# Attention scores from split fp32r operands, and output weight blocks split earlier

## The chip, the cores and the metric

One core of one Trainium2 chip runs one program. The metric is the device time of one execution in microseconds (us); lower is better. TensorE is called PE here, its weight load PEld, VectorE DVE, ScalarE ACT, GpSimd POOL and SyncE SP. In the profile's notation `128x512` is partitions by elements, `128*128` the rows and columns of the PE array that a matmul uses, and L496 is line 496 of the kernel before.

## The reference

A trunk of two layers over 512 tokens of width 1024. Each layer normalises, projects with one combined matrix, runs three mixers side by side (differential attention, a short convolution, gated linear attention), projects their concatenation with `w_out`, and adds a mixture of 16384 single-neuron experts. The change touches the differential attention and the loading of `w_out`:

```python
q, k = rope(da_q), rope(da_k)                    # (B, S, 4 heads, 2 maps, 64)
s = einsum('bqhmd,bkhmd->bhmqk', q, k) / 8       # causal
p = softmax(s)
a = p[:, :, 0] - lam * p[:, :, 1]
o = einsum('bhqk,bkhe->bqhe', a, v)              # then RMSNorm per head
...
x = x + concat([o_da, o_sc, o_g]) @ w_out        # (512, 1024) @ (1024, 1024)
x = x + peer(rmsnorm(x), ...)
```

## The kernel before

**Number formats.** Most large products are made in a split form: a float32 operand is rounded to fp32r (`hi`, a copy on ACT) and the remainder is stored in fp32r too (`lo = src - hi`, a subtraction on DVE). `split` (L88) does both. `mm3` (L82) then issues three matmuls, hi·hi, hi·lo and lo·hi. The attention scores are the exception: they are plain float32 matmuls, which the trace shows as two matmul records for each product.

**The mixer of a layer** (`mixer`, L230) streams `w_in` in slabs of 256 columns. `slab` loads four raw pieces with SP and splits each; `across` multiplies the slab with the normalised activations (48 matmuls of 512 columns) and yields two results. The last three slabs, at columns 2048, 1792 and 1536, belong to the short convolution, and the attention is written between them:

1. After gated linear attention has ended and its pool is closed, the pool `attn` opens on the right side of the memory. It holds two query tiles `qz0`, `qz1` (zeroed by POOL, L378), the exponentials `e`, their transposes `aT` and the head outputs `ho`.
2. `attend(0)`, slab 2048, `attend(1)`, slab 1792, and within slab 1536 the queries of block 2 and the first two heads of its scores.
3. The pool `wout` opens where the slabs lay. Eight blocks of 128 rows of `w_out` are loaded and split in the order 6, 7, 4, 5, 0, 1, 2, 3; `attend(2)` and `attend(3)` follow, then `out_proj` for four token blocks, each with the norm of the next stage behind it.

**Scores.** A query block `tb` of 128 tokens sees `nk = (tb+1)*128` keys. `turned_queries` (L483) copies the 64 rows of map m into `qz[r, :, m]`; the other 64 rows stay zero, so a product over all 128 rows gives the scores of one map alone. `head_weights` (L489) makes, for each of 4 heads and 2 maps, the product `qz[:, h, m]` by `kT[:, h, 0:nk]` (L496), adds the causal mask by a bfloat16 matmul over the last 128 columns (L497), takes the row maximum on DVE (L498), and exponentiates on ACT (L503). `diff_attention` (L511) transposes the difference of the maps on PE (L524), copies it out (L526) and multiplies it with the values (L528). There are 32 score products in a layer, 8 of each width 128, 256, 384 and 512.

**Order.** The program is traced in the order above and a scheduler then writes a fixed list for each engine from its own estimates of durations. Each engine works through its list in order; a matmul that waits holds up those behind it. PE interleaves slab matmuls with the attention in that list. DMAs are issued by SP (weights), by ACT, and by POOL (the rotary pieces, L469 to L481).

## Time and profile before

| | us |
|---|---|
| median of 3 runs | 2874.95 |
| lowest, highest | 2874.74, 2875.98 |
| profiled execution, whole time | 2872.9 |
| profiled execution, span of its instructions | 2871.1 |
| PE busy in it | 2844.5 |
| DVE busy in it | 2454.2 |

The profile is one execution. Its granted TensorE clock is 0.999. The attention lies at about 145 to 266 us of the span in the first layer and at about 1570 to 1691 us in the second; everything else is the slabs before it and, for the greater part of the span, the experts. A timeline row gives the start, the time from the first to the last end of a run of like instructions, the engine, the line, the operation, and how often. Because matmuls overlap, the time that one takes of PE is read from the distance of two starts.

### The profile page before, as it was taken

To read this page: it belongs to the slowest core of one execution; us is meant where nothing else is said; L and a number is where in the kernel's file an instruction comes from. 1 tells how busy PE (TensorE), PEld (TensorE's weight loads), DVE (VectorE), ACT (ScalarE), POOL (GpSimd) and SP (SyncE) were. 2 spreads that over 40 slices of the span, in tenths; PEclk is the share of its full clock that TensorE was granted. 3 is DMA by queue.
4 is the path that set the end of the run, shared out by engine and by line. 5 is a ranking of instruction groups with operands and counts; after the bars stand their busy time and mean duration, and the time that the engine had idled before them with its cause. 6 is when DMAs were issued, how large, how long until landed. Compare 5 with 4: busy or idle time off the path is not lost.

```text
span 2871.1 us, 44951 instructions
## 1 busy us (share of the span) xinstructions
PE 2844.5 (99%) x16328; PEld 2529.5 (88%) x16328; DVE 2454.2 (85%) x4874; ACT 1274.1 (44%) x1922; POOL 844.8 (29%) x715
## 2 busy tenths in 40 slices
PE   8999999999999999999999999999999999999998
PEld 7878899999998998888888788999999999988887
DVE  6675989997998899888966769999979888998888
ACT  6253346675333333333453533556743333333333
POOL 1200002211665665222112000121126665552221
PEclk9999999999999999999999999999999999999999
DMA  4322259998999999999733122699989999999995
GB/s 133 95 64 99 89 167 324 324 311 304 377 383 374 388 372 365 367 360 362 269 99 92 63 92 90 209 313 326 316 302 384 384 382 386 375 363 368 360 361 223
DMA packets 346048, 790.50 MB, mean 275 GB/s; under 512 B 32384, under 2 KB 193056, under 8 KB 341728
## 3 DMA queue, kind: packets, MB, share of 16 engines
q1 hardware_dynamic: 159472, 424.18, 40.9%
q0 software_dynamic: 87136, 312.85, 29.6%
q10 hardware_dynamic: 99216, 50.60, 5.9%
q8 instruction: 128, 2.10, 0.3%
q14 instruction: 96, 0.79, 0.1%
HBM read 705.39 MB, written 78.91 MB: 273 GB/s over the span
## 4 chain that ended last, share of the span: by engine, by line
PE 70%; DVE 4%; ACT 1%; issue 1%; DMA 0%; DVEq 0%; ACTq 0%
PE pv L85 12%; PE pv L86 12%; PE pv L84 12%; PE psh L84 8%; PE psh L85 8%; PE psh L86 8%; PE psg L1318 1%; PE psp L85 1%; PE psp L86 1%; PE psp L84 1%; PE psq L84 1%; PE psq L85 1%; PE psq L86 1%; PE pss L790 1%; PE pso L85 0%
## 5 line engine op out<-in xcount | busy, mean ns | idle before, releaser
L86 PE MATMUL pv<-vh,wl 128*128 128x512 f32 x1500 | 584.7, 390 | 0.0
L85 PE MATMUL pv<-vl,wh 128*128 128x512 f32 x1500 | 584.6, 390 | 0.0
L84 PE MATMUL pv<-vh,wh 128*128 128x512 f32 x1500 | 583.6, 389 | 0.0
L854 POOL DMA_INDIRECT row<-in_u_rows,idx x256 | 361.7, 1413 | 341.9 <-DVE row L860 224.3
L854 POOL DMA_INDIRECT row<-in_v_rows,idx x256 | 316.9, 1238 | 485.8 <-DVE yacc L867 449.7
L1020 DVE TENSOR_TENSOR vl<-vraw,vh 128x1024 fp32r<-128x1024 f32 x250 | 305.9, 1223 | 91.6 <-issue 79.1
L860 DVE SCALAR_TENSOR_TENSOR row<-row,xg 128x1024 f32<-128x1024 f32 x320 | 382.5, 1219 | 0.3 <-DMA row<-in_u_rows,idx 0.2
L1024 ACT CAST vh<-vraw 128x1024 fp32r<-128x1024 f32 x250 | 263.1, 1052 | 193.8 <-PE pv L86 184.8
L1032 ACT CAST wh<-g 128x384 fp32r<-128x384 f32 x250 | 128.3, 513 | 471.5 <-DVE g L1188 458.4
L84 PE MATMUL psh<-ahi,uwb 128*128 128x352 f32 x1024 | 334.0, 326 | 0.0
L84 PE MATMUL psh<-ahi,uwa 128*128 128x352 f32 x1024 | 333.5, 326 | 0.0
L86 PEld LDWEIGHTS pv<-vh,wl 128*128 128x128 f32 x1500 | 281.6, 188 | 58.6
L85 PEld LDWEIGHTS pv<-vl,wh 128*128 128x128 f32 x1500 | 281.6, 188 | 57.4
L84 PEld LDWEIGHTS pv<-vh,wh 128*128 128x128 f32 x1500 | 281.6, 188 | 57.3
L85 PE MATMUL psh<-alo,uwa 128*128 128x352 f32 x1024 | 330.8, 323 | 0.0
L85 PE MATMUL psh<-alo,uwb 128*128 128x352 f32 x1024 | 330.6, 323 | 0.0
L86 PE MATMUL psh<-ahi,uwa 128*128 128x352 f32 x1024 | 327.2, 320 | 0.0
L86 PE MATMUL psh<-ahi,uwb 128*128 128x352 f32 x1024 | 326.9, 319 | 0.0
L867 DVE SCALAR_TENSOR_TENSOR yacc<-row,wk,yacc 128x1024 f32<-128x1024 f32 x254 | 325.2, 1280 | 2.0
L771 ACT ACTIVATE ht<-psh 128x352 f32<-128x352 f32 x256 | 119.1, 465 | 456.6 <-PE psh L86 435.1
L756 DVE TENSOR_TENSOR uwa<-uraw,uwa 128x1024 fp32r<-128x1024 f32 x144 | 175.7, 1222 | 67.1 <-ACT uwa L755 61.2
L756 DVE TENSOR_TENSOR uwb<-uraw,uwb 128x1024 fp32r<-128x1024 f32 x144 | 175.9, 1222 | 63.0 <-ACT uwb L755 54.3
(384 smaller groups left out, 5783.0 us busy)
## 6 DMA issues: line engine op xcount, KB each, us to landing
uraw<-in_peer_u SPq DMA_DIRECT2D x256, 512.0 KB
vraw<-in_v_rows SPq DMA_DIRECT2D x252, 512.0 KB
G<-stg ACTq DMA_DIRECT2D x48, 1024.0 KB
g<-G SPq DMA_DIRECT2D x30, 1536.0 KB
H<-ht SPq DMA_DIRECT2D x144, 176.0 KB
ht<-H SPq DMA_DIRECT2D x144, 176.0 KB
wraw<-in_w_in SPq DMA_DIRECT2D x84, 256.0 KB
uraw<-in_peer_w_q SPq DMA_DIRECT2D x32, 512.0 KB
```

The source lines that it names most:

```text
L84: mm(ps, ah, bh, start=first, stop=False)
L85: mm(ps, ah, bl, start=False, stop=False)
L86: return mm(ps, al, bh, start=False, stop=last)
L756: self.before, self.last = self.last, pin(nc.vector.tensor_tensor(lo, src, hi.bitcast(F32), op=OP.subtract))
L771: pin(nc.scalar.activation(hs[c][:, 0:TD], ps, AF.Gelu))
L790: nc.tensor.matmul(pss[:, tb], qt[:, tb * P:tb * P + P], keys[:, w], start=True, stop=True)
L854: nc.gpsimd.indirect_dma_start(out=r, out_offset=None, in_=ins[name], in_offset=bass.IndirectOffsetOnAxis(ap=at, axis=0))
L860: nc.vector.scalar_tensor_tensor(r, r, 1.0, xg, op0=OP.mult, op1=OP.mult, accum_out=out)
L867: nc.vector.scalar_tensor_tensor(acc, r, w, acc, op0=OP.mult, op1=OP.add)
L1020: return pin(nc.vector.tensor_tensor(like(lo, src), src, like(hi.bitcast(F32), src), op=OP.subtract))
L1024: pin(nc.scalar.copy(vh[c], vs[c]))
L1032: pin(nc.scalar.copy(like(wh[c], ws[c]), ws[c]))
```

## The change

The scores no longer use float32 matmuls. The keys are split into `kh` (rounded, a copy on ACT) and `kl` (the remainder, on DVE). DMAs issued by POOL then stack them: after them the upper 64 rows of `kh` hold the low part of map 0's keys, and a new tile `kr` holds the rounded keys of map 1 in its upper rows and their low part in its lower rows. `turn_q` rounds the queries of a block into both halves of `qz` (copy on ACT, then a DMA into the other 64 rows) and keeps the remainder in `ql` (DVE). A score is then two fp32r matmuls and the mask: `qz[:, h, m]` (128 rows) by the stacked keys, which gives the rounded queries times rounded and low keys together, and `ql[r, h]` (64 rows) by the 64 rows of rounded keys. The zeroing of `qz` goes. Blocks 0 and 1 are turned before `attend(0)`, blocks 2 and 3 after `attend(1)`.

The key tiles and three buffers for output weight blocks lie in a new pool, `early`, with a filler tile `line` that sets where `kh` begins. The first of the three buffers serves as `kl` first. Blocks 6, 7 and 4 of `w_out` are loaded through a tile in the place of `qT` and split there, behind slab 1536 in program order; the other five go to the pool `wout`. The norm's scratch tiles take places of `attn` instead of a pool of their own.

```diff
+                kl = new_w(kp, 3).rearrange("p a (b t) -> p (a b) t", t=T)
+                kp.tile([P, 40], F32, name="line")
+                kh = kp.tile([P, 4, T], F32R, name="kh")
+                for i in range(0, 4, 2):
+                    h = slice(i, i + 2)
+                    nc.scalar.copy(kh[:, h], kT[:, h])
+                    nc.vector.tensor_tensor(kl[:, h], kT[:, h], kh[:, h].bitcast(F32), op=OP.subtract)
+                kr = mp.tile([P, 4, T], F32R, tag="kT", name="kr")
+                for i in range(0, 4, 2):
+                    h = slice(i, i + 2)
+                    nc.gpsimd.dma_start(kr[64:128, h], kh[64:128, h])
+                    nc.gpsimd.dma_start(kr[0:64, h], kl[64:128, h])
+                    nc.gpsimd.dma_start(kh[64:128, h], kl[0:64, h])
+                keys = (kh, kr)
...
+                turn_q(0)
+                turn_q(1)
                 attend(0)
...
                 attend(1)
+                turn_q(2)
+                turn_q(3)
...
+                korder = (6, 7, 4, 5, 0, 1, 2, 3)
+                wr = mp.tile([P, 2, D], F32, tag="qT", name="woraw")
+
+                def load_w(k, pool, bufs):
+                    raw = wr[:, len(wo) % 2]
+                    wo[k] = new_w(pool, bufs)
+                    nc.sync.dma_start(raw, ins["w_out"][L, k * P:(k + 1) * P, :])
+                    self.split(wo[k][:, 0], wo[k][:, 1], raw)
+
+                for k in korder[:3]:
+                    load_w(k, kp, 3)
+
             with tc.tile_pool(name="wout", bufs=1, reuse_waits="tile") as op_:
...
-                for k in korder:
-                    raw = wr.pop(0) if wr else op_.tile([P, D], F32, tag="woraw", name="woraw", bufs=2)
-                    nc.sync.dma_start(raw, ins["w_out"][L, k * P:(k + 1) * P, :])
-                    self.split(wh[:, k], wl[:, k], raw)
+                for k in korder[3:]:
+                    load_w(k, op_, 5)
...
-    def turned_queries(self, tb, qT, qz):
+    def turned_queries(self, tb, qT, qz, ql):
         s = slice(tb * P, tb * P + P)
-        for m in range(2):
-            r = slice(64 * m, 64 * m + 64)
+        rows = [slice(64 * m, 64 * m + 64) for m in range(2)]
+        for m, r in enumerate(rows):
             self.nc.scalar.copy(qz[r, :, m], qT[r, :, s])
+            self.nc.gpsimd.dma_start(qz[rows[1 - m], :, m], qz[r, :, m])
+            self.nc.vector.tensor_tensor(ql[r], qT[r, :, s], qz[r, :, m].bitcast(F32), op=OP.subtract)
...
-            nc.tensor.matmul(ps[:, 0:nk], qz[:, h, m], kT[:, h, 0:nk], start=True, stop=False)
+            r = slice(64 * m, 64 * m + 64)
+            nc.tensor.matmul(ps[:, 0:nk], qz[:, h, m], keys[m][:, h, 0:nk], start=True, stop=False)
+            nc.tensor.matmul(ps[:, 0:nk], ql[r, h], keys[m][r, h, 0:nk], start=False, stop=False)
             nc.tensor.matmul(ps[:, tb * P:nk], self.identb, self.causal, start=False, stop=True)
```

## The prediction

> **What bounds the kernel now.** I read the page first, then the busy time by stretches of the attention, then PE's timeline inside it.

> ```profile
> span 2871.1 us, 44951 instructions
> PE 2844.5 (99%) x16328; PEld 2529.5 (88%) x16328; DVE 2454.2 (85%) x4874; ACT 1274.1 (44%) x1922; POOL 844.8 (29%) x715
> ...
> 185.40:199.10 13.70, 13.08 (x61) 8.74 (x59) 9.86 (x23) 5.30 (x14) 0.00 (x0) 1.00 0.00 0
> 199.10:233.70 34.60, 34.38 (x179) 25.21 (x180) 27.13 (x67) 22.49 (x56) 0.00 (x0) 1.00 0.33 108
> ...
> sum 120.80, PE 119.91 PEld 91.31 DVE 81.44 ACT 60.38 POOL 0.51; mean PE 23.98 PEld 18.26 DVE 16.29 ACT 12.08 POOL 0.10
> ...
> sum 120.80, PE 119.76 PEld 91.01 DVE 81.35 ACT 60.16 POOL 0.51; mean PE 23.95 PEld 18.20 DVE 16.27 ACT 12.03 POOL 0.10
> ```

> The columns after the stretch are its length and the busy time of PE, PEld, DVE, ACT and POOL. The two sums are the same five stretches in the first and the second layer, from the end of gated linear attention to the first expert query. PE is busy 119.9 of 120.8 us: PE is the bound, and the stage's time is what PE's list costs. Waits can be gained only where PE is idle, 0.9 and 1.0 us a layer. So the question is what a score costs on PE before and after. Each score ends in its mask (L497), so the distance of two mask matmuls is the period of one score:

> ```profile
> 149.70 0.22 PE L497 MATMUL pss<-causal,identb 128*128 128x128 bf16 x1
> 149.76 0.44 PE L496 MATMUL pss<-kT,qz 128*128 128x128 f32 x2
> 150.03 0.22 PE L497 MATMUL pss<-causal,identb 128*128 128x128 bf16 x1
> ...
> 161.57 0.22 PE L497 MATMUL pss<-causal,identb 128*128 128x128 bf16 x1
> 161.63 0.65 PE L496 MATMUL pss<-kT,qz 128*128 128x256 f32 x2
> 162.11 0.22 PE L497 MATMUL pss<-causal,identb 128*128 128x128 bf16 x1
> ...
> 186.06 0.22 PE L497 MATMUL pss<-causal,identb 128*128 128x128 bf16 x1
> ...
> 186.81 0.22 PE L497 MATMUL pss<-causal,identb 128*128 128x128 bf16 x1
> ...
> 204.88 0.22 PE L497 MATMUL pss<-causal,identb 128*128 128x128 bf16 x1
> 204.94 1.08 PE L496 MATMUL pss<-kT,qz 128*128 128x512 f32 x2
> 205.85 0.22 PE L497 MATMUL pss<-causal,identb 128*128 128x128 bf16 x1
> ```

> The periods are 0.33, 0.54, 0.75 and 0.97 us for 1 to 4 blocks of 128 keys: 0.12 fixed (mask, and the weight load behind it that the short mask does not hide) and 0.213 per block.

> **The change part by part: a score on PE.** An fp32r matmul of known cost is that of the slabs:

> ```profile
> 135.07 0.28 PE L86 MATMUL psp<-wh,alo 128*128 128x256 f32 x1
> 135.18 0.28 PE L84 MATMUL psp<-wh,ahi 128*128 128x256 f32 x1
> ...
> 159.76 0.39 PE L84 MATMUL psp<-ahi,wh 128*128 128x512 f32 x1
> 159.99 0.39 PE L85 MATMUL psp<-alo,wh 128*128 128x512 f32 x1
> ```

> It takes 0.11 us at 256 and 0.23 at 512 columns, a quarter of float32's 0.43 and 0.85. Two passes instead of the float32 product would cost 0.107 per block of keys instead of 0.213 (at one block a weight load of about 0.11 is not covered, so nothing is gained). That alone gives periods of 0.33, 0.33, 0.44 and 0.55, a gain of 0, 0.21, 0.31 and 0.42, times 8 each 7.5 us a layer and 15.0 in all.

> But the second pass uses 64 rows of the array, the first and the mask 128. The kernel before has such neighbours in gated linear attention (psu has 64 rows, pst 128):

> ```profile
> 1508.81 1.13 PE L627 MATMUL pst<-qs,ks 128*128 128x256 f32 x4
> 1509.87 0.70 PE L665 MATMUL psu<-gv,kdT 64*128 64x256 f32 x2
> 1510.49 1.99 PE L627 MATMUL pst<-qs,ks 128*128 128x256 f32 x8
> 1512.42 0.70 PE L665 MATMUL psu<-gv,kdT 64*128 64x256 f32 x2
> 1513.04 1.13 PE L627 MATMUL pst<-qs,ks 128*128 128x256 f32 x4
> ...
> 1510.49 1.59 PEld L627 LDWEIGHTS pst<-qs,ks 128*128 128x128 f32 x8 [0.33 <-issue]
> 1512.41 0.29 PEld L665 LDWEIGHTS psu<-gv,kdT 64*128 64x128 f32 x2 [0.33 <-DVE at L629]
> ```

> Two pst products (x4 records) hold PE for 1.06 us, four (x8) for 1.93: 0.435 each and 0.19 left over for every stay in one row mode. One psu product of the same width holds it 0.62, again 0.435 and 0.19. PEld shows why: the first load after a change of mode starts only with the slot itself, while inside a mode loads run ahead. So a change of mode costs about 0.195 us, part drain, part a load that nothing covers. A new score has two, into the 64-row pass and back to the mask.

> [...]

> The mask's weights are shorter to load:

> ```profile
> L496 PEld LDWEIGHTS pss<-kT,qz 128*128 128x128 f32 x128 | 20.3, 190 | 8.2 <-issue 2.9 <-ACT e L503 2.2 <-ACT mh L553 0.5
> L497 PEld LDWEIGHTS <-identb 128*128 128x128 bf16 x64 | 6.3, 99 | 4.4 <-issue 1.9
> ```

> 99 against 190 ns, so I take 0.105 for the way back (0.195 is its upper end) and 0.30 for both. The periods become 0.53, 0.63, 0.74 and 0.85; against before +0.20, +0.09, -0.01 and -0.12, times 8 a loss of 1.3 us a layer, **+2.6** in all. With 0.195 on the way back it is 32 × 0.09 = 2.9 a layer more, +8.4; without the two changes of mode it is -15.0.

> One width has no row: no fp32r matmul here has under 256 columns. Proportional cost (nearest rows, which I take) is in the sum. The other end is the float32 cost per pass, 0.213 instead of 0.053: 2 × 0.16 × 8 = 2.6 a layer, +5.1.

> **What stands ahead of the first score.** Before, the scores began at 148.91:

> ```profile
> 144.37 1.03 PE L718 MATMUL htr<-ident,o 128*128 128x128 f32 x8
> 145.16 0.48 PE L84 MATMUL psp<-ahi,wh 128*128 128x512 f32 x1
> ...
> 148.91 0.38 PE L496 MATMUL pss<-kT,qz 128*128 128x128 f32 x2
> ...
> L89 ACT CAST woh<-woraw 128x1024 fp32r<-128x1024 f32 x16 | 16.9, 1055 | 7.3 <-DMA woraw<-in_w_out 7.2
> L90 DVE TENSOR_TENSOR wol<-woraw,woh 128x1024 fp32r<-128x1024 f32 x16 | 19.6, 1222 | 2.8 <-ACT woh L89 2.6
> L487 ACT COPY qz<-qT 64x512 f32<-64x512 f32 x16 | 9.9, 619 | 1.5 <-PE pss L496 1.2
> ...
> 100.44 2.13 POOL L481 DMA_DIRECT2D qT<-rot  x4 [12.29 <-issue]
> ...
> 106.58 1.07 POOL L469 DMA_DIRECT2D rot<-kT  x2 [2.98 <-DMA qT<-rot]
> ```

> The key tiles lie where gated linear attention lay, whose last transposes end at 145.4. Then come two copies (ACT, 1.06 each) and two subtractions (DVE, 1.22 each), of the size of L89 and L90, and six POOL DMAs of about 0.53 each to issue. The third of each three overwrites what the first reads, so it waits for that to land; POOL's queue is in order, and behind it stand the other half's three, then four for the queries of blocks 0 and 1. From the rotary rows a landing takes some 4 us (the last of four was issued near 102.0, and the next writer of the same tile started at 106.58). So the first scores come at 145.4 + 1.1 + 1.2 + 0.5 + 4 + 0.5 + 4, about 157, those of heads 2 and 3 near 161: 8 to 12 us late. PE's cover is slab 2048, 48 matmuls of 0.23 from 145.16 to 156.2, then slab 1792, 11 us more. It holds if PE's list puts slab matmuls ahead of the scores; where the scheduler thought the DMAs quicker, PE stands still for the difference, 0 to 5 us a layer. I take 1 a layer, **+2.0**.

> [...]

> **The rest, under cover.** DVE gets 8 remainders of queries (half the width of the L90 row, so about 0.61 each) and the keys' 2.4, some 7 us a layer, and ACT gets 2.1. By the sums of the stretches DVE is idle for 39 of 120.8 us and ACT for 60, so both have the room. The 3 earlier blocks move 3.7 us of DVE and 3.2 of ACT out of 199 to 234, where DVE is busy 27.1 of 34.6. What can that free? Only PE's idle time there, 0.6 us ahead of 199.1 and 0.2 after it:

> ```profile
> 199.09 0.94 PE L528 MATMUL po<-va,aT 128*128 128x128 f32 x6 [0.62 <-ACT aT L526]
> ```

> It waits for a transpose's copy, not for a block, so I take 0 and keep -0.8 a layer as the end. Three SP loads of `w_out` move ahead, waiting for the last reader of `qT`; nothing stands behind them on SP but the other blocks. Two POOL clearings go, from a queue that delays nobody. The norm's scratch in places of `attn` waits for the last exponentials, which end before the norm starts. The head outputs' tiles move down into the place of a raw block, so the second block of query weights may be split only when `out_proj` ends, one split (1.06 and 1.22 us) ahead of its use; the first block's query matmuls, 24 of 0.11 us, lie between, so I count 0. The alignment filler costs nothing by itself.

> **Sum.** +2.6 + 2.0 = +4.6 us. The sum is made against the profiled execution, 2872.9 us with 1.8 around its span; the median of the runs shown, 2874.95, lies 2.05 above it, so the forecast is 2874.95 + 4.6 = **2879.5**.

> **The rivals.** *No drain for these matmuls* (faster): in the slab stream loads run ahead of matmuls and nothing is lost, so if fp32r passes of 64 and 128 rows follow each other like that, 15.0 us go and 2.0 come: 2862. Against it: every psu slot in both layers shows the 0.19. *The narrow fp32r pass runs at float32 speed* (slower): +5.1 on the forecast, 2884.6; it decides as soon as a 128-column pass takes over 0.09 us, since 0.04 × 32 makes the 1.2 us that are missing to the bound of slower. For it: no row; against it: 0.11 at 256 columns. *PE stands at the first scores* (slower): 5 us a layer instead of 1, +8: 2887.5; it decides from 1.6 a layer. For it: the landing of 4 us; against it: 11 us of slab 1792 that could go first.

> **How the numbers follow.** About 0.2% (5.7 us) is what a measurement of this kernel can tell from no change. Forecast 0.38, its own range 2876 to 2884 (the way back at its upper end, or the idle time gained); no drain 0.30; narrow pass 0.18; stand at the first scores 0.14. Faster is the no-drain case: 0.30. Same is 0.29 of the forecast's 0.38 and 0.03 of the others. Slower is the rest, 0.38. The range goes from 2860 (no-drain without the waits) to 2888.

> **What would show it.** Right: rows of `pss` with 64*128, an idle PEld ahead of each, mask-to-mask periods near 0.63 and 0.85 at two and four blocks. Wrong: periods near 0.33 and 0.55 (no drain); fp32r pss records of one block with starts 0.2 apart (narrow pass); a PE row with several us of idle released by a DMA into `qz` or `kh` after 150 (stand). A changed pv or psh mean would show the addresses, which I price at nothing, at work.

## The result: 2895.2 us, slower, and more than the range allowed

| | before | changed |
|---|---|---|
| median, us | 2874.84 (6 runs, 2874.07 to 2875.98) | 2895.16 (6 runs, 2888.29 to 2900.25) |
| ratio, 95% interval | | 1.0069, 1.0054 to 1.0084 |
| profiled execution, whole time | 2872.9 | 2888.29 |
| mean granted clock over all its runs | 0.999 (profiled) | 0.991 to 0.996 |

The change costs 20.3 us where 4.6 were forecast; the time lies above the range's end of 2888. It also spreads over 12 us where the kernel before spreads over 2, and its three longest executions (2896.9 to 2900.3) have the lowest clocks (0.991 and 0.992). The profile of the changed kernel is its fastest execution, 15.4 us over the profiled one of before. The head of its page, and the two stretches by busy time, from the end of gated linear attention to the first expert query:

```profile
span 2886.5 us, 45042 instructions
PE 2854.1 (99%) x16328; PEld 2535.5 (88%) x16328; DVE 2460.7 (85%) x4894; ACT 1278.3 (44%) x1926; POOL 854.0 (30%) x739
```

```profile
146.11:273.20 127.09, 123.79 (x596) 93.52 (x595) 84.31 (x226) 61.90 (x162) 8.53 (x15) 0.97 0.35 91
1576.70:1705.90 129.20, 124.90 (x595) 94.47 (x594) 84.23 (x226) 61.75 (x162) 8.53 (x15) 0.96 0.34 89
```

Each stretch took 120.80 before. So 6.3 and 8.4 us of the 15.4 are in the attention, the rest in a slightly later start. PE is idle 3.3 and 4.3 us there (0.9 and 1.0 before), and the seventh column behind the stretch is new: the granted clock is 0.97 and 0.96, not 1.00. PE's timeline of the scores, layer one:

```profile
161.98 0.30 PE L528 MATMUL pss<-kh,qz 128*128 128x128 f32 x1 [0.74 <-DMA kh<-wk]
162.21 0.32 PE L529 MATMUL pss<-kh,ql 64*128 64x128 f32 x1
162.47 0.23 PE L530 MATMUL pss<-causal,identb 128*128 128x128 bf16 x1
...
163.00 0.23 PE L530 MATMUL pss<-causal,identb 128*128 128x128 bf16 x1
...
165.11 0.39 PE L84 MATMUL psp<-ahi,wh 128*128 128x512 f32 x1
167.01 0.33 PE L528 MATMUL pss<-kh,qz 128*128 128x128 f32 x1 [1.51 <-ACT e L536]
...
168.29 0.30 PE L556 MATMUL atr<-ident,e 128*128 128x128 f32 x1 [0.70 <-DVE st L538]
...
203.92 0.23 PE L530 MATMUL pss<-causal,identb 128*128 128x128 bf16 x1
...
204.68 0.23 PE L530 MATMUL pss<-causal,identb 128*128 128x128 bf16 x1
...
215.02 0.23 PE L530 MATMUL pss<-causal,identb 128*128 128x128 bf16 x1
...
215.90 0.23 PE L530 MATMUL pss<-causal,identb 128*128 128x128 bf16 x1
```

The periods, mask to mask, are 0.53, 0.76 and 0.88 for one, three and four blocks, as forecast (0.53, 0.74, 0.85). What was not forecast stands in the brackets. The first score waited for a DMA into `kh` for only 0.74; the longer waits are 1.51 for an exponential and 0.70 behind it (2.71 and 0.70 in the second layer). Why the exponential was late is in the rows of the other engines, and in the tables of DMA issues (KB each, median us to landing), of 145 to 172 us and then of two short windows, 148 to 149.5 and 155.6 to 157:

```profile
148.70 2.01 ACT L383 CAST kh<-kT 128x1024 fp32r<-128x1024 f32 x2
...
151.79 1.26 POOL L516 DMA_DIRECT2D qz<-qz  x2 [18.03 <-ACT qz L515]
153.03 0.56 POOL L388 DMA_DIRECT2D kr<-kh  x1
...
157.12 0.51 POOL L390 DMA_DIRECT2D kh<-wk  x1 [2.50 <-DMA kr<-kh]
...
164.39 0.62 ACT L89 CAST wh<-wraw 128x512 fp32r<-128x512 f32 x1 [2.84 <-DMA wraw<-in_w_in]
165.04 0.69 DVE L90 TENSOR_TENSOR wl<-wraw,wh 128x512 fp32r<-128x512 f32 x1 [2.77 <-ACT wh L89]
165.65 0.68 DVE L531 TENSOR_REDUCE st<-pss 128x1 f32<-128x128 f32 x3
166.50 0.37 ACT L536 ACTIVATE e<-pss,st 128x128 f32<-128x128 f32 x1 [1.49 <-DVE st L533]
```

```profile
wraw<-in_w_in SPq DMA_DIRECT2D x5, 256.0 KB, 3.3
qz<-qz POOLq DMA_DIRECT2D x4, 128.0 KB, 4.0
kr<-kh POOLq DMA_DIRECT2D x2, 256.0 KB, 4.6
kr<-wk POOLq DMA_DIRECT2D x2, 256.0 KB, 5.4
kh<-wk POOLq DMA_DIRECT2D x2, 256.0 KB, 5.1
```

```profile
wraw<-in_w_in SPq DMA_DIRECT2D x2, 256.0 KB, 2.9
```

```profile
wraw<-in_w_in SPq DMA_DIRECT2D x1, 256.0 KB, 5.2
```

The masks of the first four scores had started by 164.1, but DVE's list holds the split of a raw weight piece of slab 1536 ahead of the row maxima. The raw pieces landed late beside the keys' DMAs: those issued ahead of them took 2.9 us, the one issued among them 5.2 (in the second layer 5.0 and 6.9), and the last piece was cast only at 164.39. DVE came to the maxima at 165.65, the exponentials began at 166.50, and PE, whose four score buffers were full, stood until 167.01. Then the clock, in three windows of 3.41 us:

```profile
162.63:166.05 3.42, 2.87 (x15) 1.88 (x14) 1.01 (x4) 0.62 (x1) 0.00 (x0) 1.00 1.43 148
166.05:169.46 3.41, 1.75 (x11) 1.33 (x11) 2.29 (x12) 1.77 (x9) 0.00 (x0) 1.00 0.00 0
169.46:172.88 3.42, 3.42 (x14) 2.44 (x13) 1.32 (x7) 2.55 (x8) 0.61 (x1) 0.50 0.00 0
```

The granted clock falls from 1.00 to 0.50 at 169.46 and stays there 6.8 us; in the second layer it is 10.2 us. Slab matmuls of 512 columns start 0.43 us apart there (at 174.37 and 174.80) instead of 0.23. At most half of that time is lost, 8.5. Of the 14.7 us in the two stretches 5.7 are more idle time and 3.7 the periods (worked out below), so some 5.3 are left for the half clock. The spread says that slower executions lose more to it.

### The profile page after: what moved, and what is told of

Read it like the earlier page. It is cut to its first block, busy times and chain, and to the rows that moved or that the text cites. A ratio compares the mean times of both kernels' runs of the same rounds, so it can differ in the third digit from the quotient of the medians.

```text
span 2886.5 us, 45042 instructions
## 1 busy us (share of the span) xinstructions
PE 2854.1 (99%) x16328; PEld 2535.5 (88%) x16328; DVE 2460.7 (85%) x4894; ACT 1278.3 (44%) x1926; POOL 854.0 (30%) x739
## 4 chain that ended last, share of the span: by engine, by line
PE 90%; DVE 7%; issue 1%; ACT 1%; DMA 1%; SPq 0%; DVEq 0%; ACTq 0%
PE pv L86 12%; PE pv L85 12%; PE pv L84 12%; PE psh L84 10%; PE psh L85 10%; PE psh L86 10%; PE psp L85 2%; PE psp L86 2%; PE psp L84 2%; PE psg L1350 2%; PE psq L85 2%; PE psq L84 2%; PE psq L86 2%; PE pss L822 1%; PE pso L85 1%
## 5 line engine op out<-in xcount | busy, mean ns | idle before, releaser
L86 PE MATMUL pv<-vh,wl 128*128 128x512 f32 x1500 | 584.7, 390 | 0.0
L85 PE MATMUL pv<-vl,wh 128*128 128x512 f32 x1500 | 584.6, 390 | 0.0
L84 PE MATMUL pv<-vh,wh 128*128 128x512 f32 x1500 | 583.7, 389 | 0.0
L84 PE MATMUL psh<-ahi,uwb 128*128 128x352 f32 x1024 | 334.0, 326 | 0.0
L84 PE MATMUL psh<-ahi,uwa 128*128 128x352 f32 x1024 | 333.8, 326 | 0.0
L86 PEld LDWEIGHTS pv<-vh,wl 128*128 128x128 f32 x1500 | 281.5, 188 | 58.6
L85 PEld LDWEIGHTS pv<-vl,wh 128*128 128x128 f32 x1500 | 281.5, 188 | 57.7
L84 PEld LDWEIGHTS pv<-vh,wh 128*128 128x128 f32 x1500 | 281.6, 188 | 57.1
L85 PE MATMUL psh<-alo,uwb 128*128 128x352 f32 x1024 | 330.8, 323 | 0.0
L85 PE MATMUL psh<-alo,uwa 128*128 128x352 f32 x1024 | 330.6, 323 | 0.0
L86 PE MATMUL psh<-ahi,uwa 128*128 128x352 f32 x1024 | 327.3, 320 | 0.0
L86 PE MATMUL psh<-ahi,uwb 128*128 128x352 f32 x1024 | 326.9, 319 | 0.0
L788 DVE TENSOR_TENSOR uwa<-uraw,uwa 128x1024 fp32r<-128x1024 f32 x144 | 175.8, 1222 | 74.8 <-ACT uwa L787 74.6
L788 DVE TENSOR_TENSOR uwb<-uraw,uwb 128x1024 fp32r<-128x1024 f32 x144 | 175.9, 1222 | 57.8 <-ACT uwb L787 57.6
```

What stands on the lines that cost most here:

```text
L84: mm(ps, ah, bh, start=first, stop=False)
L85: mm(ps, ah, bl, start=False, stop=False)
L86: return mm(ps, al, bh, start=False, stop=last)
L788: self.before, self.last = self.last, pin(nc.vector.tensor_tensor(lo, src, hi.bitcast(F32), op=OP.subtract))
```

## The experiments

"Idle" is the sum of PE's waits over 0.15 us in 140 to 300 and in 1560 to 1720 us, first and second layer; "half clock" the time at granted clock 0.50 there. Both are of one profiled execution, the times of all runs. The medians of the kernel before, measured again beside each group of runs, lie between 2874.8 and 2875.8.

| kernel | median us | ratio, 95% interval | idle us | half clock us |
|---|---|---|---|---|
| before | 2874.8 | 1 | 1.1, 1.1 | 0, 0 |
| changed | 2895.2 | 1.0069 (1.0054, 1.0084) | 3.4, 4.5 | 6.8, 10.2 |
| changed, once more | 2898.1 | 1.0072 (1.0057, 1.0087) | 3.2, 3.2 | 20.5, 23.9 |
| old scores, rest of the change | 2873.1 | 0.9992 (0.9983, 1.0002) | 0.7, 0.8 | 0, 0 |
| attention a slab later | 2893.0 | 1.0064 (1.0048, 1.0081) | 6.0, 5.4 | 6.8, 6.8 |
| second pass over 128 rows | 2875.4 | 1.0001 (0.9992, 1.0011) | 5.2, 5.5 | 6.8, 6.8 |
| both of these | 2880.0 | 1.0016 (1.0006, 1.0025) | 7.8, 7.6 | 6.8, 10.2 |
| no DMAs | 2880.6 | 1.0020 (1.0011, 1.0030) | 1.2, 1.0 | 0, 0 |
| DVE's order | 2886.1 | 1.0038 (1.0025, 1.0052) | 2.1, 1.6 | 13.7, 3.4 |
| DVE's order, 128 rows | 2868.2 | 0.9975 (0.9965, 0.9984) | 4.0, 3.9 | 0, 0 |
| no DMAs, 128 rows | 2866.8 | 0.9971 (0.9960, 0.9982) | 3.1, 3.2 | 3.4, 0 |
| the same, queries later | 2865.2 | 0.9965 (0.9952, 0.9978) | 2.9, 2.8 | 0, 0 |
| the same, copy on POOL | 2870.8 | 0.9985 (0.9976, 0.9993) | 3.4, 3.0 | 3.4, 6.8 |
| before + a wait in slab 2048 | 2888.8 | 1.0047 (1.0031, 1.0062) | 4.8, 6.4 | 6.8, 6.8 |
| before + a wait behind slab 2048 | 2892.0 | 1.0058 (1.0041, 1.0075) | 6.4, 6.6 | 6.8, 6.8 |
| that wait, wide matmuls in it | 2887.8 | 1.0039 (1.0025, 1.0053) | 3.1, 2.2 | 0, 0 |
| that wait, narrow matmuls in it | 2891.6 | 1.0056 (1.0040, 1.0073) | 1.5, 1.5 | 6.8, 6.8 |

The first theory was that PE runs out of score buffers because the scores of blocks 0 and 1 are bunched in its list, with late raw weights and dear passes as rivals.

**Attention a slab later.**

```diff
-                attend(0)
                 ...
                 for j, ps in across(2048):
                     nc.scalar.copy(z[:, j, 2:], ps)
-                attend(1)
+                attend(0)
                 ...
                 for j, ps in across(1792):
                     nc.vector.tensor_tensor(z[:, j, 2:], ps, z[:, j, 2:], op=OP.mult)
+                attend(1)
```

> The changed kernel with the attention of token blocks 0 and 1 written one slab later (block 0 behind slab 2048, block 1 behind slab 1792); keys, queries and their DMAs stay where they are. The changed kernel's profile has 3.4 and 4.5 us of PE idle a layer at the first scores and then 7 and 10 us at half clock. Theory 'bunching' (scores of blocks 0 and 1 stand back to back in PE's list, PE runs out of score buffers and waits for DVE and ACT): slab matmuls now stand between them, idle falls to about 1 us a layer, no half clock, time 2877 to 2881. Rival 'late raw weights' (the key DMAs delay slab 1536's raw pieces, DVE's list stands behind their split, whatever stands in PE's list): idle stays over 2 us a layer, the clock still falls, 2886 to 2900. Theory 'it is the passes' (idle is a small part): within 3 us of the changed kernel.

2893.0 us: the bunching theory fell. PE waited 1.69 for the same exponential, and two waits of 1.70 for the residual additions came late in the stage. Slab matmuls between the scores did not help here, where the softmax itself was late. The run doesn't decide between the other two: its time is within 3 us of the changed kernel, and PE still waits over 2 us a layer.

**Second pass over 128 rows**, alone and with the edit above.

```diff
-            nc.tensor.matmul(ps[:, 0:nk], ql[r, h], keys[m][r, h, 0:nk], start=False, stop=False)
+            nc.tensor.matmul(ps[:, 0:nk], ql[:, h], keys[m][:, h, 0:nk], start=False, stop=False)
```

> The changed kernel with the second score pass over all 128 rows (ql[:, h] by keys[m][:, h]) instead of 64; the other 64 rows add low query times low key of the other map, of the size of the product of low parts that is left out anyway. If the change of row mode costs what the prediction took: periods of a score 0.33, 0.33, 0.44, 0.55 instead of 0.53, 0.63, 0.75, 0.87, which is 17.6 to 19 us less in all, if nothing else takes it up: 2871 to 2880. If the idle at the first scores comes from score buffers, shorter scores run into it sooner and part of the gain is lost: 2878 to 2890, PE idle over 5 us a layer. If the row mode is not what makes the pass dear: periods as before, within 3 us of the changed kernel.

> Both edits: attention of blocks 0 and 1 one slab later, and the second pass over 128 rows. If idle and row mode are the two costs and they add: 2859 to 2863, which is 12 to 16 us under the kernel before. If the freed time only turns into waiting for softmax and raw pieces: 2868 to 2880.

The other 64 rows bring in products of a low query and a low key of the two maps, as small as the product of low parts that the split form leaves out anyway. The first is 2875.4, 19.7 us under the changed kernel. Its masks:

```profile
162.09 0.23 PE L529 MATMUL pss<-causal,identb 128*128 128x128 bf16 x1
...
162.40 0.23 PE L529 MATMUL pss<-causal,identb 128*128 128x128 bf16 x1
```

The period of one block is 0.30 instead of 0.53, so the two changes of row mode were what made it long, by 0.23. The gain is 2 us more than the 17.6 of the prediction's periods, although idle time grew to 5.2 and 5.5 us; the clock is part of the gain, 0.996 to 0.997 in all its executions against 0.991 to 0.996. The combination came to 2880.0: the freed time turned into waiting, as its second case had it.

**No DMAs.**

```diff
-                    nc.scalar.copy(kh[:, h], kT[:, h])
-                    nc.vector.tensor_tensor(kl[:, h], kT[:, h], kh[:, h].bitcast(F32), op=OP.subtract)
...
-                    nc.gpsimd.dma_start(kr[64:128, h], kh[64:128, h])
-                    nc.gpsimd.dma_start(kr[0:64, h], kl[64:128, h])
-                    nc.gpsimd.dma_start(kh[64:128, h], kl[0:64, h])
+                    nc.scalar.copy(kh[lo, h], kT[lo, h])
+                    nc.vector.tensor_tensor(kh[up, h], kT[lo, h], kh[lo, h].bitcast(F32), op=OP.subtract)
+                    nc.scalar.copy(kl[up, h], kT[up, h])
+                    nc.vector.tensor_tensor(kl[lo, h], kT[up, h], kl[up, h].bitcast(F32), op=OP.subtract)
...
+                    nc.scalar.copy(kr[:, h], kl[:, h].bitcast(F32))
...
-            self.nc.gpsimd.dma_start(qz[rows[1 - m], :, m], qz[r, :, m])
+            self.nc.scalar.copy(qz[rows[1 - m], :, m], qT[r, :, s])
```

> The changed kernel without its POOL DMAs: keys and queries are stacked by ACT copies and DVE subtractions that write to the other 64 partitions; the stacked keys of map 1 are built in the buffer of kl and copied to their place by ACT (2 copies of 128x1024 a layer more); the 64-row pass stays. First scores at about 152 instead of 162 us. Theory that the late DMAs are the cause (of the first scores' wait and of the raw pieces' delay): idle at the first scores under 1.2 us a layer, no half clock, time 2876 to 2881, which is the forecast without its wait. Rival 'bunching' (softmax chain against score buffers, with or without DMAs): idle stays at 2 us a layer or more, 2884 or more.

The median of 2880.6 us is within 1.1 of the forecast of 2879.5 by luck. It lies between two groups of five executions, 2877.0 to 2878.7 with a mean clock of 0.999 and 2882.5 to 2884.2 with 0.998, and the forecast holds a wait of 2.0 that isn't there. The profiled execution, the fastest, has the idle time of before, the clock at 1.00, and a span of 2874.8, 3.7 over before: without DMAs, and where the clock holds, the change costs what the periods say. The measured periods (0.53, 0.65, 0.76, 0.88 against 0.33, 0.54, 0.75, 0.97) give 16 × (0.20 + 0.11 + 0.01 − 0.09) = 3.7. The slower group has no trace. Its times are about 5 us longer and its clock is lower, so a half clock that comes in some executions is the likely reason, and it comes without the keys' DMAs.

**DVE's order**: the splits of slab 1536 issue behind the row maxima of block 0.

```diff
+                red = self.red.ins                      # the last row maximum of attend(0)
-                for j, ps in across(1536):
+                gen = across(1536)
+                def behind():
+                    with tc.issue_after(red):
+                        first = next(gen)
+                    yield first
+                    yield from gen
+                for j, ps in behind():
```

> The changed kernel with one order changed: on DVE the four remainder splits of slab 1536 stand behind the row maxima of token block 0 instead of ahead of them. DMAs and PE's list up to the second pair of scores as they were. Theory 'DVE's list stands behind a late raw piece': the waits of PE for exponentials, 1.5 and 2.7 us, go below 0.8; the half clock goes or shortens; 2876 to 2886. Rival 'late keys are enough': PE still waits for keys of heads 2 and 3 and for score buffers, the clock still halves, 2887 to 2900.

The waits for exponentials are gone, so the late piece in DVE's list was their cause. 9.1 us of the change's 20.3 went with them. But the clock fell all the same, for 13.7 and 3.4 us, and here PE was not idle:

```profile
1596.44:1599.86 3.42, 3.27 (x17) 2.24 (x17) 2.34 (x11) 1.88 (x9) 0.00 (x0) 1.00 0.41 35
1599.86:1603.27 3.41, 3.41 (x21) 2.36 (x20) 2.02 (x9) 2.19 (x7) 0.44 (x1) 1.00 0.00 0
1603.27:1606.68 3.41, 3.41 (x10) 2.26 (x9) 1.54 (x7) 1.57 (x8) 0.78 (x2) 0.50 0.55 77
```

```profile
1602.39 0.23 PE L539 MATMUL pss<-causal,identb 128*128 128x128 bf16 x1
...
1603.04 0.23 PE L539 MATMUL pss<-causal,identb 128*128 128x128 bf16 x1
```

The rows are two windows at full clock and the one behind them, then two masks of adjacent scores of two blocks. The window ahead of the fall is busy for 3.41 of 3.41 us. So busy time isn't what keeps the clock. The theory was changed to: what counts is how much PE streams. At 0.23 us for 512 columns a score of one block streams 384 columns, an estimate of 0.17 us, in a period of 0.53: a share of 0.32. For two blocks (period 0.65, the two masks above) it is 0.44, for three and four 0.53 and 0.59, and over 128 rows 0.17 in 0.30, 0.57.

**The clock by itself**, on the kernel before. First a wait in slab 2048, then in a place where nothing else is left to do, bare and with 20 matmuls in it. The diff shows the second place; the first has `z[:, 0]` instead of `z[:, 1]`, behind the first half of the slab, and no added matmuls:

```diff
                 for j, ps in across(2048):
                     nc.scalar.copy(z[:, j, 2:], ps)
+                w1, w2 = (ap.tile([P, 64], F32, name=n, bufs=1) for n in ("w1", "w2"))
+                nc.gpsimd.dma_start(w1, z[:, 1, 2:66])
+                nc.gpsimd.dma_start(w2, w1)
+                for k in range(20):                     # wide; narrow: hh[r, ...], 128 columns, r of 64 and 128 rows in turn
+                    f = nc.tensor.matmul(psf, hh[:, 0, 0:P], hh[:, 1], start=True, stop=True)
+                    mc.enter_context(tc.issue_after(f.ins))
+                psw = self.psA.tile([P, T], F32, tag="a", name="psw")
+                mc.enter_context(tc.issue_after(nc.tensor.transpose(psw[0:64, 0:P], w2, self.ident).ins))
```

> The kernel before with nothing changed but a wait: in each layer, after the first half of slab 2048, 64 columns of its result go through two POOL DMAs, and PE's list stands behind a transpose of them (its result is not used). PE idles there some 4 to 6 us with everything else as before. Theory 'idle time halves the clock': behind each wait the granted clock is 0.50 for 3.4, 6.8 or 10.2 us (the lengths seen so far), which costs half of that again: in all 8 to 12 us of idle and 3.4 to 10 us of half clock, 2887 to 2897, with a spread from run to run of several us. Rival 'the half clock comes from the narrow passes or the row mode': clock 1.00 throughout, 2883 to 2887, spread as before (under 2 us).

> The kernel before plus a wait in another place than the first stall: behind the end of slab 2048, where no attention is left over; 64 columns of its result go through two POOL DMAs and PE's list stands behind a transpose of them (result unused). PE is idle 4 to 6 us a layer. Theory 'columns streamed': half clock of 3.4 to 6.8 us a layer, total 12 to 18 us over before, 2887 to 2893. Rival 'only waiting costs': the idle alone, 2883 to 2887.

> The same wait, with 20 fp32r matmuls of 512 columns (4.6 us, result unused) in PE's list ahead of the transpose that waits. The wait lasts as long, PE works through it. Theory 'columns streamed': the clock stays at 1.00 and only the wait is paid: 8 to 11 us over before, 4 to 7 us less than the bare wait, 2883 to 2887. Rival (no such effect): the same time as the bare wait, within 2 us.

> The same wait with 20 fp32r matmuls of 128 columns that change the row mode each time (64, 128, 64 rows; some 4.7 us; result unused). PE is busy by the profile but streams a quarter of the time. Theory 'columns streamed': the clock falls as in the bare wait, 2887 to 2893. Rival 'a busy PE keeps its clock': as with the wide matmuls, 2883 to 2887.

The kernel with the first wait has 9.0 us more idle time, 4.9 of them at the waits themselves (1.9 and 3.0, shorter than expected), and 13.7 at half clock; 9.0 + 6.8 is the 15.8 by which the span grew. There is no narrow pass in that kernel. The second wait by windows and by PE's timeline: bare, then wide, then narrow.

```profile
164.78:168.20 3.42, 0.00 (x0) 0.00 (x0) 2.31 (x4) 1.20 (x3) 1.12 (x2) 1.00 0.33 86
168.20:171.61 3.41, 2.28 (x8) 1.55 (x8) 1.12 (x2) 0.62 (x1) 0.00 (x0) 0.50 0.04 10
```

```profile
169.33 0.42 PE L393 MATMUL psw<-ident,w 128*64 128x128 f32 x1 [5.30 <-DMA w<-w]
```

```profile
163.69 4.70 PE L394 MATMUL psf<-ahi 128*128 128x512 f32 x20
169.17 0.30 PE L397 MATMUL psw<-ident,w 128*64 128x128 f32 x1 [0.79 <-DMA w<-w]
```

```profile
164.85:168.26 3.41, 3.41 (x16) 2.60 (x14) 2.07 (x4) 0.96 (x2) 1.13 (x2) 1.00 0.31 87
168.26:171.68 3.42, 2.63 (x15) 1.93 (x15) 2.10 (x6) 1.03 (x3) 0.00 (x0) 1.00 0.03 10
```

```profile
162.20 6.35 PE L395 MATMUL psf<-ahi 64*128 64x128 f32 x20
168.35 0.41 PE L398 MATMUL psw<-ident,w 128*64 128x128 f32 x1
```

```profile
161.77:165.18 3.41, 3.41 (x15) 2.28 (x13) 3.20 (x10) 2.14 (x4) 0.57 (x1) 1.00 0.04 11
165.18:168.59 3.41, 3.41 (x11) 2.52 (x11) 0.84 (x2) 0.62 (x1) 0.55 (x1) 0.50 0.32 85
```

In the first layer the transpose starts 5.0 us after ACT begins the copy of `z`, both bare and with wide matmuls. The narrow ones took 6.35, partly at half clock, and with them it starts after 5.75. Wide matmuls keep the clock and save 4.2 us; narrow ones that change the row mode keep PE just as busy, lose the clock, and save 0.4. So in these three kernels the clock went with streaming and not with busy time, and the bare wait cost more than its idle time: 16.3 us by the medians (2892.0 against 2875.75 beside it) for 10.8 us more idle (13.0 against 2.2). Whether columns alone count, or columns times rows, these runs don't separate: half of the narrow ones use 64 rows. Nor is the change of row mode tried apart from the width.

**DVE's order and 128 rows together.**

> Two edits to the changed kernel: DVE's order (splits of slab 1536 behind the row maxima of block 0) and the second pass over all 128 rows. With DVE's order alone PE was busy 3.27 and 3.41 of 3.41 us in the windows ahead of the halving, yet the clock fell, for 13.7 and 3.4 us. Theory 'columns streamed count, not busy time': a score of 128 keys streams about 0.16 us of columns in 0.53 us with the row modes and in 0.33 us without, so without them the share is about a half, the clock stays at 1.00 or falls once at most, and the time is 2864 to 2871. Rival 'the DMAs or the late start bring the half clock': it still falls for 6.8 us or more a layer, 2871 to 2878.

2868.2 us: the DMAs stay, the scores start as late (162.3), and the clock stays at 1.00. The rival that the DMAs or the late start bring the half clock fell. Taking the row modes out is worth 17.9 us here and 13.8 without DMAs.

**The rest of the change** (float32 scores of before, all else as changed).

> All of the change except the scores: the float32 score product of the kernel before (qz zeroed by POOL for each block), no stacked keys, but the three early w_out blocks, their raw pieces in the place of qT, and the norm's scratch in places of attn. The prediction priced these at 0 with an end of -0.8 a layer. By it 2873.5 to 2875.5, same as before, full clock throughout. If the early blocks or the addresses are a cost of their own: above 2877.

2873.1 us, no different from before: early blocks and addresses are free, as priced.

**No DMAs and 128 rows; then the queries of block 1 later; then the copy of the stacked keys on POOL.**

```diff
-                turn_q(1)
                 attend(0)
+                with tc.issue_after(self.exps[3].ins):  # the exponentials of the second head
+                    turn_q(1)
...
-                    nc.scalar.copy(kr[:, h], kl[:, h].bitcast(F32))
+                    nc.gpsimd.tensor_copy(kr[:, h], kl[:, h].bitcast(F32))
```

> Keys and queries stacked by ACT and DVE without POOL DMAs, and the second pass over 128 rows. The version without DMAs came to 1.002 of the kernel before (2880.6); the passes over 128 rows should take 17.6 to 19 us from it if the row mode is all that the pass costs above the prediction's narrow case: 2862 to 2864, 0.9955 of before. If shorter scores run out of score buffers (softmax on DVE and ACT cannot keep up), PE idles at 150 to 200 us and half or more is lost: 2870 to 2876.

> No POOL DMAs, second pass over 128 rows (2866.8 us), and the queries of block 1 are rounded only behind the exponentials of block 0's second head instead of ahead of them. In the version it starts from PE waits 1.3 us a layer for exponentials that stand behind four query copies of 0.62 us on ACT and a remainder of 0.69 us on DVE, and the clock falls once for 3.4 us. If that order is the cause: idle at 160 us under 0.5, clock 1.00, 2862 to 2865. If the score buffers run out anyway: within 1.5 us of 2866.8.

> The same, with the stacked keys of map 1 copied to their place by POOL instead of ACT (2 copies of 128x1024 a layer). If ACT's 2 us in front of the exponentials matter: another 1 to 2 us less, 2861 to 2864. If POOL's copy is slow or disturbs DVE: scores of map 1 come late, same or up to 4 us more.

The first is 2866.8, 3 to 5 us above the 2862 to 2864 expected: PE waited 1.32 at the same exponentials. With the queries later the waits there are 0.69 and 0.40, not under the 0.5 expected, but the clock holds: 2865.2, ratio 0.9965 (0.9952 to 0.9978), which beats both kernels; that it beats the first of the three is not shown, since the intervals overlap. POOL's copy is a loss of 5.6 us: it takes 3.01 for two where ACT took 2.00, and beside it DVE's two query remainders took 2.13 instead of 1.40. PE's idle time grew by only 0.7; the 10.2 us at half clock that came with it cost up to 5.1, so the loss is for the most part the clock. The rows are of the POOL version, then of the one it started with:

```profile
155.87 2.13 DVE L520 TENSOR_TENSOR ql<-qT,qz 64x512 fp32r<-64x512 f32 x2
155.90 3.01 POOL L391 CAST kr<-wk 128x1024 fp32r<-128x1024 f32 x2 [21.24 <-DVE wk L387]
```

```profile
154.51 1.40 DVE L520 TENSOR_TENSOR ql<-qT,qz 64x512 fp32r<-64x512 f32 x2
```

**The changed kernel once more.**

> The changed kernel itself, on another chip and day: its runs so far lie between 2888 and 2900 us with a mean granted clock of 0.996 to 0.991. Theory 'columns streamed, decided in windows that run free of the program': again a spread of 5 us or more, the slower the lower the clock, and PE's idle time of the new profile within 2 us of the first (3.4 and 4.5 us). Rival 'the DMAs land at different times': idle time differs by more than 3 us between profiles.

```profile
166.45:169.86 3.41, 2.00 (x12) 1.51 (x12) 2.23 (x12) 1.77 (x10) 0.00 (x0) 1.00 0.00 0
169.86:173.27 3.41, 3.41 (x13) 2.32 (x12) 1.37 (x8) 2.94 (x11) 0.98 (x2) 0.50 0.00 0
...
186.93:190.34 3.41, 3.41 (x12) 2.83 (x11) 3.38 (x16) 1.24 (x4) 1.22 (x2) 0.50 0.44 61
190.34:193.75 3.41, 3.41 (x17) 2.78 (x16) 1.87 (x5) 0.00 (x0) 0.00 (x0) 1.00 0.58 172
```

This execution took 2898.8, its span 10.5 us over the first profile's. It was idle 1.5 us less and at half clock for 44.4 us instead of 17.1. The difference between the two is the half clock, not the DMAs. Why it lasts is the author's reading and not shown: the scores of few columns that follow run at half clock too (10 to 13 matmuls in a window of 3.41 us, 17 in the first one at full clock, from 190.34) and keep the share low. Nor is it shown that the windows run free of the program: the fall stands at 169.46 in the first profile and at 169.86 in this one.

## Why the prediction was wrong, point by point

- **Row modes: right.** The periods were forecast within 0.03 us (+2.6, measured 3.7), so the rival "no drain" is out. So is "narrow pass at float32 speed": two such passes and a mask take 0.30 us without row modes, where two passes at 0.213 alone would take 0.43. That the pass costs just 0.053 is not shown, nor that the way back costs 0.105 by itself: the two changes of mode cost 0.23 together at one block, where the prediction's periods have 0.20. Nor is it shown how the 0.195 of one change splits between a drain and the load; in its rows PEld stood idle for 0.33 us ahead of each first load.
- **The rest under cover: right for the early blocks and addresses,** which cost nothing. DVE and ACT had room in the sums, but the place of an instruction in DVE's list decided.
- **The failed step is "what stands ahead of the first score".** It put the first scores near 157 and the wait at 1 us a layer, +2.0. They came at 161.98. The landings are not why: from the first key DMA to the first score are 8.95 us, and the prediction counts 0.5 + 4 + 0.5 + 4. That DMA was issued at 153.03 and not near 147.7, since ACT's list had other work ahead of the key copies (148.70 instead of 145.4) and POOL's list had two DMAs of queries first. PE's list had slab matmuls for nearly all of the delay, and the wait itself, 0.74 and 0.57, was below what was taken. Two things were missing. The keys' DMAs delay the raw weights (5.2 us to landing among them, 2.9 ahead of them), which the prediction left out, and DVE's list carries that delay into the softmax: 9.1 us with the clock that hung on it, by the run with DVE's order. And time on PE was taken as the only price, where a stretch that streams little halves the clock behind it: 17.1 us at half clock in the fastest execution, 44.4 in a slower one.
- **The rival "PE stands at the first scores"** (2887.5) named the right place, but not the mechanism: it needed 5 us of waiting a layer for keys, and PE waited 2.2 and 3.4 us behind the softmax. Its time was 7.7 us short, and it had no clock in it.
- **The landing time.** The prediction took some 4 us from the rotary rows; the keys' rows say 4.6 to 5.4 us for 256 KB beside the weights' loads.

## What to carry to other kernels

Price a stretch of small matmuls not only by its time but by the share of it in which columns stream: where that sank below about 0.4 for 3.4 us (an estimate, last section), whether through waiting or through narrow matmuls that change the row mode, the clock halved here for 3.4 us or a multiple. Where two operands share the array rows, take all 128 rows if what the unwanted half adds is below the error already accepted: one line gave 13 to 20 us here. And when DMAs are added, follow the transfers they delay to the in-order list whose next instruction somebody needs.
